# Swap, rope and split of dilated queries and keys by projection halves, with swap transfers issued by two engines

## The chip, the cores and the metric

One core of one Trainium2 chip runs the whole program. The metric is the device time of one execution, in microseconds. TensorE multiplies matrices into PSUM, VectorE and ScalarE work on rows of up to 128 partitions, GpSimd does the same more slowly, and SyncE does nothing here but issue transfers (ScalarE may issue them too).

## The reference, cut to what matters

Two layers run one after the other on 1024 tokens of width 1024. The second one has, beside a latent attention, a dilated one with 24 heads in three groups of 8. The change is in how its queries and keys are prepared:

```python
DIL_CONFIGS = ((128, 1), (512, 4), (2048, 16))      # window, dilation of group g

def rope(t, positions):
    ...
    t1, t2 = t[..., : dim // 2], t[..., dim // 2:]
    rot = jnp.concatenate([-t2, t1], axis=-1)
    return t * cos + rot * sin

def dilated_mixture(q, k, v, positions):
    q = rope(q.reshape(B, S, DIL_HEADS, DIL_HEAD_DIM), positions)
    k = rope(k.reshape(B, S, DIL_HEADS, DIL_HEAD_DIM), positions)
    ...
    for g, (window, dilation) in enumerate(DIL_CONFIGS):
        o, lse = dilated_group(q[:, :, sl], k[:, :, sl], v[:, :, sl], dilation, window // (2 * dilation))
    ...
    alpha = jax.nn.softmax(jnp.stack(lses, axis=0), axis=0)
    out = jnp.sum(alpha[..., None] * outs, axis=0)
```

Group g sees the tokens sorted by their remainder modulo the dilation (1, 4, 16), each remainder a band of its own. The head width is 64.

## The kernel before

All products are in float32 precision, made of three products of float32r parts: an operand is split into a high part (`hi`, a cast by ScalarE) and the rest (`lo`, a subtraction by VectorE, `sub_lo` in line 119). A projection of 128 channels by 512 tokens is 24 matmuls (lines 360 to 362), which need no other engine while they run.

The dilated stage is twelve units, g outermost: units 0 to 3 are g = 0, 4 to 7 are g = 1, 8 to 11 are g = 2. A unit is two heads, 128 channels on the partitions. Its three items in the stream of projections are key, query and value, each in two halves of 512 tokens. `q_evac` and `k_evac` take such a half out of PSUM; `ordered` copies it on ScalarE into the tile `rt` (128 x 1024), with the tokens sorted by remainder for g > 0 (half 0 and half 1 then interleave in blocks of 512 / dilation columns). After the second half, `roped` runs on the whole tile: four transfers copy `rt` with its 32-partition blocks exchanged in pairs into `rsw`, and VectorE computes rt * cos + rsw * sin in three steps. `split2` then casts and subtracts for each of the two heads (64 partitions each), into `qs` or `ksd`; for the keys two more transfers copy `ksd` onto the other 64 partitions. After this the scores of the unit (lines 1179, 1180) may run.

What sets the order: TensorE's instructions are put in order by a planner in the kernel (class `Flow`). It has lanes for scores (`score_lane`), transposes (`turn_lane`), values (`value_lane`) and the stream of projections, and each step of a lane waits for planned times: a lane is taken up when its events have come by the planner's own costs. `F.chain(("v", 1.3), ...)` adds a VectorE step of 1.3 us to the plan, and returns its end, which becomes `kev.t` or `qev.t`, the events that the scores of the unit wait for. Transfers cost SWAP = 4.5 us from the copy on, whichever engine issues them. The other engines' instructions are put in order by the framework's scheduler. The tiles `rt` and `rsw` come from a pool of six (`C`, with the planner's ring `R.C`), `qs` and `ksd` from pools of three.

All transfers signal their end on eight semaphores that go round (DMAHW0 to DMAHW7): one that is to use a semaphore first waits, on the engine that issues it, until the one before on that semaphore has landed.

Of the kernel before, what the change touches and what calls it, by code (L numbers as in the profile page):

```python
# [8 lines left out]
F32R = mybir.dt.float32r  # L9
# [5 lines left out]
S = 1024  # L15
# [52 lines left out]
def hybrid_kernel(  # L68
# [46 lines left out]
    def C(name="c", dt=F32):  # L115
        return cp.tile([128, 1024], dt, tag="c", name=name)
# [1049 lines left out]
    class Unit:  # L1166


        def __init__(self, j, g):
            self.j, self.g = j, g  # L1170
            self.kev, self.qev, self.vev = Ev(), Ev(), Ev()
            self.heads = [self.head(i) for i in range(2)]

# [33 lines left out]

        def roped(self, box, ps, half):

            if not half:  # L1210
                if self.j == 0 and not hasattr(self, "ks"):
                    tabs[0] = tables(self.g)
                box += [C("rt"), R.C.take()]
            t = box[0]
            e = self.ordered(t, ps, half)
            if half:
                cosT, sinT = tabs[0]
                sw, slot = C("rsw"), R.C.take()
                for b in range(4):
                    nc.sync.dma_start(sw[32 * b:32 * b + 32], t[32 * (b ^ 1):32 * (b ^ 1) + 32])  # L1220
                nc.vector.tensor_tensor(out=sw, in0=sw, in1=sinT, op=ALU.mult)  # L1221
                nc.vector.tensor_tensor(out=t, in0=t, in1=cosT, op=ALU.mult)
                nc.vector.tensor_tensor(out=t, in0=t, in1=sw, op=ALU.add)
                slot.t = F.chain(("v", 1.3), ("v", 1.3), ("v", 1.3), at=e + SWAP)
                box.append(slot.t)
            return e

        def split2(self, dst, t, at):

            for i in range(2):  # L1230
                r = slice(64 * i, 64 * i + 64)
                hi, lo = dst(i)
                nc.scalar.copy(hi, t[r])
                sub_lo(nc.vector, lo, t[r], hi)
            return F.chain(("a", 1.1), ("v", 1.3), ("v", 1.3), at=at)

        def q_evac(self):
            box = []

            def f(half):  # L1240
                def g(ps):
                    e = self.roped(box, ps, half)
                    if half:
                        self.qs = [dq.tile([128, S], F32R, tag="qs", name="qs") for i in range(2)]
                        self.qev.t = self.split2(lambda i: (self.qs[i][64 * i:64 * i + 64], self.qs[i][64 - 64 * i:128 - 64 * i]), box[0], box[2])
                        box[1].t = self.qev.t
                    return e
                return g
            return f

        def k_evac(self):
            box = []

            def f(half):
                def g(ps):
                    e = self.roped(box, ps, half)
                    if half:
                        self.ks = [dq.tile([128, 2, S], F32R, tag="ks", name="ksd") for i in range(2)]
                        t = self.split2(lambda i: [self.ks[i][64 * i:64 * i + 64, n] for n in range(2)], box[0], box[2])
                        for i in range(2):  # L1260
                            nc.sync.dma_start(self.ks[i][64 - 64 * i:128 - 64 * i].bitcast(F32), self.ks[i][64 * i:64 * i + 64].bitcast(F32))
                        box[1].t = t
                        self.kev.t = t + 4.0
                    return e
                return g
            return f
# [619 lines left out]
```

## Time and profile before

| | us |
|---|---|
| median of 3 runs | 1724.4 |
| lowest, highest of them | 1714.8, 1727.25 |
| the profiled execution, its own time | 1715.64 |
| its span in the trace | 1713.8 |
| TensorE busy | 1643.7 |
| VectorE, ScalarE busy | 980.1, 769.3 |

The profile is of one execution, and what lies between its span and its time is 1.8 us. A TensorE that is busy is not one at its peak; where it is idle, the profile names the engine and the line that ended the wait last. The dilated stage lies between about 417 and 1016 us.

### The profile page before, as it was taken

What the parts mean: (1) busy time and instruction counts of PE and PEld (TensorE: products, weight loads), DVE (VectorE), ACT (ScalarE), POOL (GpSimd) and SP (SyncE); (2) the same over time, 40 slices, a digit from 0 to 9 for tenths busy, and PEclk for the clock granted to TensorE, in tenths of its full rate; (3) what the DMA queues carried; (4) which work ended last, traced back from release to release, by engine and by line L of the source; (5) the groups of instructions that cost most, each with busy time, mean ns of one, the idle gap of its engine ahead of it and who ended that gap; (6) DMA issues with size and microseconds to landing.
All of it is one profiled execution on the core that took longest, in us unless ns stands there. A gap on an engine that the chain in (4) does not pass through costs nothing.

```text
span 1713.8 us, 22215 instructions
## 1 busy us (share of the span) xinstructions
PE 1643.7 (96%) x7988; PEld 1354.5 (79%) x7988; DVE 980.1 (57%) x1875; ACT 769.3 (45%) x1611; POOL 235.9 (14%) x224
## 2 busy tenths in 40 slices
PE   6999998999999899999999989999999999999998
PEld 6888876788788788888888777888777777777886
DVE  6487694553565656666555563374556566435433
ACT  5365524332455546555454542214566555632121
POOL 2000020000000010000000444451112122012200
PEclk8999999999999999999999999999999999999999
DMA  6211224534433343444334668455314132378542
GB/s 190 56 50 39 69 87 131 173 111 135 98 94 87 84 111 85 99 96 120 94 91 111 165 172 225 91 163 156 101 46 114 51 105 70 96 258 268 173 136 76
DMA packets 216090, 200.52 MB, mean 117 GB/s; under 512 B 49779, under 2 KB 180211, under 8 KB 214444
## 3 DMA queue, kind: packets, MB, share of 16 engines
q1 hardware_dynamic: 212844, 188.55, 40.0%
q10 hardware_dynamic: 3136, 10.55, 1.9%
q8 instruction: 63, 1.03, 0.3%
q14 instruction: 47, 0.39, 0.1%
HBM read 124.70 MB, written 48.07 MB: 101 GB/s over the span
## 4 chain that ended last, share of the span: by engine, by line
PE 70%; DMA 10%; DVE 6%; SPq 4%; ACT 4%; issue 3%; POOL 2%; DVEq 0%; POOLq 0%; ACTq 0%
PE pp L360 12%; PE pp L361 12%; PE pp L362 12%; PE y L361 3%; PE y L362 3%; PE y L360 3%; PE pso L493 3%; DMA rsw<-rt 3%; PE pst L463 2%; SPq L1220 2%; PE pso L1698 2%; PE pss L1655 2%; PE pso L1684 2%; PE pss L1657 2%; PE pss L1656 2%
## 5 line engine op out<-in xcount | busy, mean ns | idle before, releaser
L360 PE MATMUL pp<-Hh,whi 128*128 128x512 f32 x1248 | 503.7, 404 | 10.2 <-DVE pg L594 4.5
L361 PE MATMUL pp<-Hl,whi 128*128 128x512 f32 x1248 | 491.1, 394 | 0.0
L362 PE MATMUL pp<-Hh,wlo 128*128 128x512 f32 x1248 | 490.7, 393 | 0.0
L360 PEld LDWEIGHTS pp<-Hh,whi 128*128 128x128 f32 x1248 | 237.6, 190 | 56.7 <-DVE pg L594 5.5
L362 PEld LDWEIGHTS pp<-Hh,wlo 128*128 128x128 f32 x1248 | 236.5, 190 | 52.1
L361 PEld LDWEIGHTS pp<-Hl,whi 128*128 128x128 f32 x1248 | 237.4, 190 | 41.9
L119 DVE TENSOR_TENSOR wlo<-wraw,whi 128x1024 fp32r<-128x1024 f32 (+1 forms) x108 | 131.3, 1215 | 100.6 <-ACT whi L127 95.4
L127 ACT CAST whi<-wraw 128x1024 fp32r<-128x1024 f32 (+1 forms) x108 | 109.1, 1010 | 174.4 <-PE pp L361 77.3
L443 ACT ACTIVATE P<-P,nm 128x256 f32<-128x256 f32 (+2 forms) x256 | 118.6, 466 | 58.9 <-DVE nm L438 58.5
L119 DVE TENSOR_TENSOR pl<-pss,E 128x512 fp32r<-128x512 f32 x128 | 86.3, 688 | 91.5 <-ACT E L1663 91.0
L1662 ACT ACTIVATE pss<-pss 128x512 f32<-128x512 f32 x128 | 74.1, 582 | 111.4 <-PE pss L1657 102.2
L1599 DVE TENSOR_REDUCE mx<-pst 128x1 f32<-128x512 f32 x128 | 82.7, 684 | 32.0 <-PE pst L1597 31.5
L119 DVE TENSOR_TENSOR pl<-pst,ph 128x512 fp32r<-128x512 f32 (+2 forms) x120 | 75.2, 638 | 33.1 <-ACT ph L469 32.5
L432 DVE CUSTOM_DVE_ANT_0 P<-pss,cc 128x256 f32<-128x256 f32 (+2 forms) x192 | 63.0, 369 | 44.3 <-PE pss L1180 44.2
L469 ACT CAST ph<-pst 128x512 fp32r<-128x512 f32 (+2 forms) x120 | 63.8, 550 | 32.9 <-PE pst L463 31.9
L1663 ACT CAST E<-pss 128x512 fp32r<-128x512 f32 x128 | 72.8, 586 | 1.9
L493 PE MATMUL pso<-pl,v 128*128 128x256 f32 (+1 forms) x280 | 71.0, 284 | 2.3 <-DVE pl L119 2.3
L1221 DVE TENSOR_TENSOR rsw<-rsw,tab 128x1024 f32<-128x1024 f32 x24 | 29.4, 1224 | 73.1 <-DMA rsw<-rt 73.1
L493 PE MATMUL pso<-ph,v 128*128 128x256 f32 (+1 forms) x280 | 71.0, 283 | 0.2 <-ACT ph L469 0.2
L463 PE MATMUL pst<-idt,P 128*128 128x128 f32 x440 | 67.4, 274 | 2.6 <-ACT P L443 2.3
L502 ACT COPY ot<-pso 64x512 f32<-64x512 f32 x64 | 37.4, 584 | 70.2 <-PE pso L493 69.5
L1179 PE MATMUL pss<-ksd,qs 128*128 128x256 f32 (+2 forms) x192 | 50.0, 287 | 15.2 <-DVE qs L119 15.2
(262 smaller groups left out, 2999.1 us busy)
## 6 DMA issues: line engine op xcount, KB each, us to landing
wraw<-in_w_in_dram SPq DMA_DIRECT2D x78, 512.0 KB
rsw<-rt SPq DMA_DIRECT2D x96, 128.0 KB
ksd<-ksd SPq DMA_DIRECT2D x24, 512.0 KB
wraw<-in_w_out_dram SPq DMA_DIRECT2D x16, 512.0 KB
g_d<-g ACTq DMA_DIRECT2D x16, 512.0 KB
og_d<-ot SPq DMA_DIRECT2D x48, 128.0 KB
ol<-og_d SPq DMA_DIRECT2D x24, 256.0 KB
ol<-b_d SPq DMA_DIRECT2D x48, 128.0 KB
```

Of the source, the lines that this page charges most:

```text
L119: eng.tensor_tensor(out=lo, in0=src, in1=hi.bitcast(F32), op=ALU.subtract)
L127: nc.scalar.copy(wh, raw)
L360: nc.tensor.matmul(ps, lh, rh, start=(i == 0), stop=False)
L361: nc.tensor.matmul(ps, lh, rl, start=False, stop=False)
L362: nc.tensor.matmul(ps, ll, rh, start=False, stop=(i == n - 1))
L443: nc.scalar.activation(out=a, in_=a, func=AF.Exp, bias=nm[:, i:i + 1], scale=hd.scale, accum_out=hd.den[:, i:i + 1])
L463: nc.tensor.transpose(ps[:, w:w + 128], hd.P[i // 4][:, i % 4, p0:p0 + 128], ident)
L469: nc.scalar.copy(ph[:, :w], ps[:, :w])
L493: nc.tensor.matmul(o[b][:, q0:q0 + 128 * w], hd.v(c), part[:, cols + 128 * x:cols + 128 * (x + w)], start=b not in opened, stop=(part is p ...
L1599: nc.vector.tensor_reduce(out=mx[:, n, i:i + 1], in_=ps, axis=mybir.AxisListType.X, op=ALU.max)
L1662: nc.scalar.activation(out=ps, in_=ps, func=AF.Exp, scale=MSC)
L1663: nc.scalar.copy(ph, ps)
```

## The change

For g = 0 and g = 1 (`by_half`), everything that `roped` and `split2` do is done for each half as soon as that half has been copied: transfers of 32 x 512 in place of 32 x 1024, VectorE's and ScalarE's steps on 512 columns (`places` picks the half's columns; for g = 1 these are four blocks of 128). `rsw`, `qs` and `ksd` are taken at the first half. The planner's costs of the steps become 0.7 in place of 1.1 and 1.3. For g = 2 the whole tile is handled as before. For all three groups the four transfers of a swap are issued by SyncE and ScalarE by turns. The copies of `ksd` onto the other partitions stay as they were, after the second half.

```diff
--- before.py
+++ after.py
@@ -1167,7 +1167,7 @@
 
 
         def __init__(self, j, g):
-            self.j, self.g = j, g
+            self.j, self.g, self.by_half = j, g, g < 2
             self.kev, self.qev, self.vev = Ev(), Ev(), Ev()
             self.heads = [self.head(i) for i in range(2)]
 
@@ -1207,32 +1207,47 @@
 
         def roped(self, box, ps, half):
 
+
             if not half:
                 if self.j == 0 and not hasattr(self, "ks"):
                     tabs[0] = tables(self.g)
                 box += [C("rt"), R.C.take()]
             t = box[0]
             e = self.ordered(t, ps, half)
-            if half:
+            if self.by_half and not half or half and not self.by_half:
+                box += [C("rsw"), R.C.take()]
+            if half or self.by_half:
+                sw, v = box[2], self.places(half)
+                for b in range(4):
+                    (nc.sync, nc.scalar)[b % 2].dma_start(v(sw[32 * b:32 * b + 32]), v(t[32 * (b ^ 1):32 * (b ^ 1) + 32]))
                 cosT, sinT = tabs[0]
-                sw, slot = C("rsw"), R.C.take()
-                for b in range(4):
-                    nc.sync.dma_start(sw[32 * b:32 * b + 32], t[32 * (b ^ 1):32 * (b ^ 1) + 32])
-                nc.vector.tensor_tensor(out=sw, in0=sw, in1=sinT, op=ALU.mult)
-                nc.vector.tensor_tensor(out=t, in0=t, in1=cosT, op=ALU.mult)
-                nc.vector.tensor_tensor(out=t, in0=t, in1=sw, op=ALU.add)
-                slot.t = F.chain(("v", 1.3), ("v", 1.3), ("v", 1.3), at=e + SWAP)
-                box.append(slot.t)
+                nc.vector.tensor_tensor(out=v(sw), in0=v(sw), in1=v(sinT), op=ALU.mult)
+                nc.vector.tensor_tensor(out=v(t), in0=v(t), in1=v(cosT), op=ALU.mult)
+                nc.vector.tensor_tensor(out=v(t), in0=v(t), in1=v(sw), op=ALU.add)
+                us = 0.7 if self.by_half else 1.3
+                at = F.chain(("v", us), ("v", us), ("v", us), at=e + SWAP)
+                if half:
+                    box[3].t = at
+                box.append(at)
             return e
 
-        def split2(self, dst, t, at):
-
+        def places(self, half):
+
+            if not self.by_half:
+                return lambda ap: ap
+            m = 512 // RES[self.g]
+            return lambda ap: grouped(ap, self.g)[:, :, m * half:m * half + m] if self.g else ap[:, tokens(half)]
+
+        def split2(self, dst, t, at, half):
+
+            v = self.places(half)
             for i in range(2):
                 r = slice(64 * i, 64 * i + 64)
                 hi, lo = dst(i)
-                nc.scalar.copy(hi, t[r])
-                sub_lo(nc.vector, lo, t[r], hi)
-            return F.chain(("a", 1.1), ("v", 1.3), ("v", 1.3), at=at)
+                nc.scalar.copy(v(hi), v(t[r]))
+                sub_lo(nc.vector, v(lo), v(t[r]), v(hi))
+            us = 0.7 if self.by_half else 1.3
+            return F.chain(("a", us), ("v", us), ("v", us), at=at)
 
         def q_evac(self):
             box = []
@@ -1240,10 +1255,12 @@
             def f(half):
                 def g(ps):
                     e = self.roped(box, ps, half)
+                    if half == (not self.by_half):
+                        self.qs = [dq.tile([128, S], F32R, tag="qs", name="qs") for i in range(2)]
+                    if half or self.by_half:
+                        t = self.split2(lambda i: (self.qs[i][64 * i:64 * i + 64], self.qs[i][64 - 64 * i:128 - 64 * i]), box[0], box[-1], half)
                     if half:
-                        self.qs = [dq.tile([128, S], F32R, tag="qs", name="qs") for i in range(2)]
-                        self.qev.t = self.split2(lambda i: (self.qs[i][64 * i:64 * i + 64], self.qs[i][64 - 64 * i:128 - 64 * i]), box[0], box[2])
-                        box[1].t = self.qev.t
+                        self.qev.t = box[1].t = t
                     return e
                 return g
             return f
@@ -1254,9 +1271,11 @@
             def f(half):
                 def g(ps):
                     e = self.roped(box, ps, half)
+                    if half == (not self.by_half):
+                        self.ks = [dq.tile([128, 2, S], F32R, tag="ks", name="ksd") for i in range(2)]
+                    if half or self.by_half:
+                        t = self.split2(lambda i: [self.ks[i][64 * i:64 * i + 64, n] for n in range(2)], box[0], box[-1], half)
                     if half:
-                        self.ks = [dq.tile([128, 2, S], F32R, tag="ks", name="ksd") for i in range(2)]
-                        t = self.split2(lambda i: [self.ks[i][64 * i:64 * i + 64, n] for n in range(2)], box[0], box[2])
                         for i in range(2):
                             nc.sync.dma_start(self.ks[i][64 - 64 * i:128 - 64 * i].bitcast(F32), self.ks[i][64 * i:64 * i + 64].bitcast(F32))
                         box[1].t = t
```

In the order of TensorE, the first place that moves is unit 0: what stands ahead of its first scores (`pss<-ksd,qs`), the end of a projection of the next unit and the transposes of values (`pst<-idt,vt`).

```order
-L360 MATMUL pp<-Hh,whi 128x512
-L361 MATMUL pp<-Hl,whi 128x512
-L362 MATMUL pp<-Hh,wlo 128x512
-L518 MATMUL pst<-idt,vt 128x128 x8
 L1179 MATMUL pss<-ksd,qs 128x192
 L1180 MATMUL pss<-ksd,qs 128x192
```

Four more groups of three matmuls ahead of the rows shown go the same way: the scores move up past 15 matmuls of a projection and the 8 transposes, which now come later. In unit 3, 36 wide matmuls (384 or 512 columns) and 22 narrower ones stand between the query's second half and the first scores before, and 21 and 23 now.

On ScalarE, the second half of unit 3's queries: from the copy out of PSUM (`rt<-pp`) to the casts of the split (`qs<-rt`), with the high parts of P (`ph`), an output (`ot`) and the values' copy (`vt`) between. Before:

```order
L1205 COPY rt<-pp 128x512
L502 COPY ot<-pso 64x512
L469 CAST ph<-pst 128x512 x3
L1280 COPY vt<-pp 128x512
L1233 CAST qs<-rt 64x1024 x2
L502 COPY ot<-pso 64x512
L469 CAST ph<-pst 128x128
```

and now:

```order
L1205 COPY rt<-pp 128x512
L469 CAST ph<-pst 128x512
L1222 DMA rsw<-rt 32x512 x2
L469 CAST ph<-pst 128x512
L502 COPY ot<-pso 64x512
L469 CAST ph<-pst 128x128
L1299 COPY vt<-pp 128x512
L469 CAST ph<-pst 128x384
L1247 CAST qs<-rt 64x512 x2
```

Two transfers come in behind the copy, and the casts are of the second half alone (those of the first half stand ahead of this piece).

On SyncE, the key tile of unit 11 (g = 2): `st_d` and `cx` are the store and the twelve reads of the statistics of unit 10's heads, `d_d` the store of a merged output, which waits for GpSimd. Before, with the semaphores that a row waits for:

```order
L1320 DMA st_d<-sT 96x128 [waits DMAHW2_49,Activation_49]
L1384 DMA d_d<-acc 128x1024 [waits DMAHW3_49,Pool_49]
L1220 DMA rsw<-rt 32x1024 [waits DMAHW4_49,Activation_49]
L1220 DMA rsw<-rt 32x1024 [waits DMAHW5_49]
L1220 DMA rsw<-rt 32x1024 [waits DMAHW6_49]
L1220 DMA rsw<-rt 32x1024 [waits DMAHW7_49]
L1334 DMA cx<-st_d 16x64 [waits DMAHW2_49,DMAHW0_49]
L1337 DMA cx<-st_d 16x4x16 [waits DMAHW1_49]
```

and now:

```order
L1356 DMA cx<-st_d 16x16x4 [waits DMAHW0_49]
L1353 DMA cx<-st_d 16x64 [waits DMAHW1_49]
L1356 DMA cx<-st_d 16x4x16
L1403 DMA d_d<-acc 128x1024 [waits DMAHW3_49,Pool_49]
L1356 DMA cx<-st_d 16x16x4 [waits DMAHW4_49]
L1353 DMA cx<-st_d 16x64 [waits DMAHW5_49]
L1356 DMA cx<-st_d 16x4x16 [waits DMAHW6_49]
L1356 DMA cx<-st_d 16x16x4 [waits DMAHW7_49]
L1222 DMA rsw<-rt 32x1024 [waits DMAHW1_49,Activation_49]
L1222 DMA rsw<-rt 32x1024 [waits DMAHW3_49]
```

Ahead of the second piece stand the store of the statistics and five more reads. The swap has gone behind all twelve reads and the store of the output, and is two transfers. ScalarE's order at the same place, now:

```order
L1203 COPY rt<-pp 128x16x32 [waits PE_49]
L469 CAST ph<-pst 128x512 [waits PE_49]
L1222 DMA rsw<-rt 32x1024 [waits DMAHW2_49,DMAHW3_49,DMAHW1_49,DMAHW4_49,DMAHW0_49,DMAHW7_49,Activation_49,Pool_49]
L1222 DMA rsw<-rt 32x1024 [waits DMAHW2_49]
L443 ACTIVATE P,st<-P,nm 128x128 [waits DVE_49]
```

The other two transfers of the swap stand here, and wait for DMAHW0 and DMAHW2, the semaphores of the sixth and the eighth read.

## Rows read from the trace of the kernel before

**Rows 1.** The page, part 1: busy us, share of the span, instructions

```profile
PE 1643.7 (96%) x7988; PEld 1354.5 (79%) x7988; DVE 980.1 (57%) x1875; ACT 769.3 (45%) x1611; POOL 235.9 (14%) x224
```

**Rows 2.** Waits of TensorE, 410 to 815 us: us, times, longest us

```profile
PE pss L1179 <- DVE qs L119: 8.0, 4, 3.9
PE pst L518 <- ACT vt L1283: 2.3, 1, 2.3
```

**Rows 3.** The same, 815 to 1020 us

```profile
PE pss L1179 <- DVE qs L119: 7.3, 3, 3.8
...
PE pso L493 <- DVE pl L119: 1.1, 1, 1.1
```

**Rows 4.** Windows of 25 us: busy us (instructions) by engine, PEclk, DMA, GB/s

```profile
400.00:425.00 25.00, 25.00 (x115) 20.53 (x115) 7.74 (x10) 6.60 (x11) 0.71 (x2) 1.00 0.38 110
575.00:600.00 25.00, 20.74 (x102) 17.85 (x103) 13.57 (x31) 10.72 (x28) 0.15 (x1) 0.86 0.27 64
...
975.00:1000.00 25.00, 21.08 (x102) 17.42 (x102) 18.53 (x32) 11.64 (x22) 5.06 (x7) 0.93 0.79 188
```

**Rows 5.** Chain of waits, 573 to 590 us: start us, us, what

```profile
573.10 0.58 ACT rt L1205
...
574.30 1.51 SPq L1220
...
576.49 4.34 DMA rsw<-rt
...
580.95 1.22 DVE rsw L1221
...
583.91 1.14 DVE rt L1223
...
585.13 1.05 ACT qs L1233
...
586.20 1.23 DVE qs L119
...
587.48 0.53 PE pss L1179
```

**Rows 6.** Chain of waits, 410 to 1020 us

```profile
431.14 2.32 DMA rsw<-rt
...
485.98 1.16 PE pso L493 x10
...
971.77 1.81 DMA cx<-st_d
```

**Rows 7.** Tile rt: SyncE's swap transfers, duration ns min/median/max

```profile
L1220 SPq DMA_DIRECT2D rsw<-rt x96: 512/588/2192, 429.2 to 984.6; - x96
```

**Rows 8.** Tile g: transfers issued by ScalarE, duration ns min/median/max

```profile
L1048 ACTq DMA_DIRECT2D g_d<-g x16: 321/326/348, 1115.2 to 1525.9; - x16
```

**Rows 9.** VectorE by line and shape, 420 to 1016 us: count, busy, mean ns, idle before

```profile
L119 DVE TENSOR_TENSOR pl<-pst,ph 128x512 fp32r<-128x512 f32 x70 | 47.2, 683 | 27.6 <-ACT ph L469 27.5
...
L119 DVE TENSOR_TENSOR qs<-rt,qs 64x1024 fp32r<-64x1024 f32 x24 | 30.3, 1261 | 12.6 <-ACT qs L1233 12.2
...
L1221 DVE TENSOR_TENSOR rsw<-rsw,tab 128x1024 f32<-128x1024 f32 x24 | 29.4, 1224 | 73.1 <-DMA rsw<-rt 73.1
```

**Rows 10.** ScalarE by line and shape, 420 to 1016 us

```profile
L502 ACT COPY ot<-pso 64x512 f32<-64x512 f32 x45 | 26.3, 584 | 48.9 <-PE pso L493 48.4
...
L1233 ACT CAST qs<-rt 64x1024 fp32r<-64x1024 f32 x24 | 25.1, 1045 | 66.3 <-DVE rt L1223 66.0
```

**Rows 11.** Timeline of SyncE's transfers, 905 to 970 us

```profile
912.13 0.34 SPq L1334 DMA_DIRECT2D cx<-st_d  x1
...
916.34 0.89 SPq L1337 DMA_DIRECT2D cx<-st_d  x2
...
957.42 0.38 SPq L1320 DMA_DIRECT2D st_d<-sT  x1
```

## The prediction

> **What bounds the kernel now.** The page's first part comes first: TensorE is busy for 1643.7 of 1713.8 us [rows 1], so all that any change of order can win is the 70.1 us in which it stands, and what its clock loses. The change touches only the dilated stage, from about 417 us (first projection of its keys) to 1016 us. So I read TensorE's own waits there, apart for the two first groups of the units (g = 0 and 1, units 0 to 7, to 815 us) and the last one (g = 2, units 8 to 11). In both one wait leads: the first scores of a unit wait for VectorE's last step on the queries, 8.0 us in four waits and 7.3 us in three [rows 2, 3]. The rest of each list is short (2.3 us for the values, 1.1 us for a low part). The third view is the clock: of its two levels, 2.4 and 1.2 GHz, the lower was granted for part of the stretches around the longest of these waits (mean 0.86 in 575 to 600 us, 0.93 in 975 to 1000 and likewise in 850 to 875) [rows 4]. 25 us times the missing shares is 3.5 + 1.75 + 1.75 = 7.0 us at most. So what is to be won is 15.3 + 7.0 = 22.3 us, 1.3% of the time.
>
> Then the chain of such a wait, in unit 3 [rows 5]: ScalarE ends the copy of the second half at 573.68; SyncE issues four swap transfers until 576.49 (one took 1.51 us); they are there for VectorE 4.34 us later; three VectorE steps on 1024 columns end at 585.05; ScalarE's cast 1.05, VectorE's subtraction 1.23; the scores start at 587.48, 13.8 us after the copy. TensorE's cover for these 13.8 us is the work that stands between the projection and the scores. In the order before that is 36 matmuls of 384 to 512 columns and 22 narrower ones in unit 3. At 25.00 us for 115 wide ones [rows 4] and 1.16 us for ten narrow ones [rows 6] it is 36 x 0.22 + 22 x 0.116 = 10.5 us. The lack of 3.3 us beside the 3.9 us wait [rows 2] says that this reckoning holds. Counted in the same way, the cover of the 12 units before is 16.1, 16.8, 11.8, 10.5, 15.5, 15.3, 16.4, 15.1 and, for g = 2, 15.1, 14.2, 18.0, 16.2 us.
>
> **The change, part by part.**
>
> *The chain in halves (units 0 to 7).* For a half, the transfers on each queue are two: 2 x 0.59 = 1.2 us of issue by the median of the swap's own transfers [rows 7]. Landing: between 2.32 and 4.34 us after the last issue [rows 6, 5]. VectorE on 512 columns: no row shows it with both operands in SBUF; the same operation with one operand in PSUM takes 683 ns at 512, against 1224 and 1261 ns at 1024 [rows 9]; bounds 0.61 (half of 1224) and 0.68, and I take 0.68, a row of the operation itself. Three of them 2.05, up to 0.6 of other work between (the three of unit 3 took 4.1 us for 3.6 of work [rows 5]). Cast 0.58 [rows 10], subtraction 0.68, hops 0.3. Sum: 1.2 + 2.3 + 2.05 + 0.58 + 0.68 + 0.3 = 7.1 us to 1.2 + 4.3 + 2.65 + 1.56 = 9.7 us, in place of 13.8.
>
> *The order of TensorE* moves with it, since the planner reckons with the shorter steps: it puts scores earlier, and so takes away cover. The count in the new order gives 11.9, 13.7, 12.1, 7.3, 11.8, 13.7, 14.3, 14.3 us for units 0 to 7. Against 7.1 to 9.7 only unit 3 can still wait, 0 to 2.4 us; I take 1.0. Of the 8.0 us 7.0 go.
>
> *Two queues for all units.* For g = 2 halves are not used, so here only the issue changes: 1.2 us instead of four transfers, of which one in a query tile is held to about 2.2 us (maximum 2.192 [rows 7]). The cover becomes 15.3, 15.7, 15.7, 15.7, while issue falls by 1.2 to 3.5 us. Of the 7.3 us I take 6.0 as gone; the 3.8 us one had a cover that my reckoning calls nearly enough already, and may have another reason.
>
> The Trainium skill speaks against this part: "DMA: Bandwidth & Descriptors", section "Issuing engines are not separate DMA queues", says that a second issuing engine saves only the sequencer's own time, which is usually small beside the transfer. Here the traced issue is not small (1.51 us for one of four transfers beside 4.34 us of landing [rows 5]); by the rule the landing stays, as in my sum; what it would do to the held transfers is a rival below.
>
> *Clock.* If these waits go, so do most of the low stretches: 5.0 of 7.0 us, as unit 3's may stay in part. Gain so far: 7.0 + 6.0 + 5.0 = 18 us.
>
> *What ScalarE pays.* 80 transfers are now issued by ScalarE (64 for units 0 to 7, 16 for g = 2). Its own issue takes 0.326 us, SyncE's of the same swap 0.588 [rows 8, 7]: 26 to 47 us more in some 600, on an engine that is busy for 45% of the span [rows 1]. The halved casts are 32 more instructions, 16 x 2 x (2 x 0.584 - 1.05) = 4 us [rows 10, 5]. What hides this: ScalarE already stands 66.3 us in front of the query casts, waiting for VectorE [rows 10], with everything behind it, and the longest that TensorE waits for ScalarE is 2.3 us [rows 2]. Queued behind a transfer are the copies out of PSUM, the exponentials and the high parts of P. The bounds are 0 and 26 us (every one of 80 issues, 0.326 each, straight into TensorE). The nearest rows are the small waits that stand there today, so I take 4.
>
> *Transfers that ScalarE must wait for.* All transfers share eight completion semaphores (DMAHW0 to 7) in turn, and a transfer waits until the last one on its semaphore has landed. Until now that wait was SyncE's; now half of it stands in ScalarE's order. In most places the earlier transfer is over 5 us back. The exception is the key tile of units 10 and 11, where the twelve small statistics reads (cx) are issued just ahead: ScalarE waits for the sixth and eighth of them. In unit 10 the first read went out at 912.13 and the eighth by 916.8 [rows 11]; one lands 1.81 us after its issue [rows 6]. So ScalarE can be held there for 918.6 - 912.1 = 6.5 us if its copy is done when the reads start, and for nothing if it comes late; unit 11, whose statistics left at 957.42 [rows 11], has the same steps. Of this TensorE hides at least the 24 matmuls (5.3 us) that fill its other projection bank. Bounds 0 and 2 x 6.5 = 13; I take 3, what is left when the half of it is hidden and the copy comes midway.
>
> *VectorE* gets 5 x 16 = 80 more instructions, 16 x 5 x (2 x 0.683 - 1.22) = 12 us more work in 600, beside 73.1 us in which it stands today for swap transfers [rows 9]. It will stand for them 40 times instead of 24. Bounds 0 and 5 us of TensorE; 1 taken, since its waits for VectorE's other results are short today (1.1 us) [rows 3]. SyncE loses 16 transfers: nothing.
>
> **The sum.** 18 - 4 - 3 - 1 = 10 us gained. The profiled execution took 1715.6 us (span 1713.8), so 1705.6 for one like it; it lies near the lower end of the three runs shown, whose median is 1724.4. Against the median: 1724.4 - 10 = 1714 us. A measurement of this kernel tells about 1% (17 us) from no change.
>
> **Rivals.**
> *1. ScalarE becomes the late engine (slower).* Its order is fixed; a swap transfer stands in it that waits for its copy, for the tile's last readers and for a semaphore that another transfer, still stuck in SyncE's queue, has to free. There are 40 pairs. If each costs TensorE 0.7 us (the issue of both, 2 x 0.326), that is 26 us, with two more low-clock stretches of 3.5 us it is 33, against a gain of 15: 1724.4 + 18 = 1742; range 1728 to 1755. For it: the copies out of PSUM are ScalarE's, and the planner counts no time for the transfers. Against it: the 66.3 us that ScalarE stands today [rows 10] with almost no harm. It decides from 18 us of new TensorE waits on.
> *2. The cover shrinks as fast as the chain (no change).* If the chain is nearer 11 to 13 us (the landing of smaller transfers not shorter, VectorE's steps held by other work), units 0, 2, 3 and 4 wait again, since their cover is 7.3 to 12.1: 1724, range 1719 to 1730. For it: in unit 3 cover goes from 10.5 to 7.3.
> *3. The queue change gives only issue time.* Held transfers (2.192 us) stay held, since all run on the same engines; g = 2 keeps about 4 of its 7.3 us and 3.5 us of clock: 1714 + 5 = 1719. This is what the skill's rule would make of it; no row can show it before.
> *4. All of it, and ScalarE pays nothing:* 1724.4 - 22 = 1702.
>
> **How the numbers follow.** Forecast (1707 to 1722) 0.45; rival 3, beside it, 0.13; rival 2 0.12; rival 1 0.18; rival 4 0.12. Slower by over 1% (above 1741) is over half of rival 1: 0.10; faster by over 1% (under 1707) is rival 4 and a tail of the forecast: 0.20; the rest 0.70. The range runs from 1697 (rival 4, with a run as low as those of before go) to 1738 (the middle of rival 1).
>
> **What would show it.** Right: TensorE's waits of scores on the queries fall from 15.3 us to under 4; copy to first score in unit 3 under 11 us; no low clock near that place; transfers on ScalarE of 0.3 to 0.6 us; TensorE's busy time unchanged. Wrong: new waits of TensorE on ScalarE's copies, exponentials or high parts over 10 us in sum, or ScalarE idle in front of swap transfers by more than 20 us; scores that still wait on queries in units 0, 2 or 4; swap transfers on SyncE still held to 2 us.

## The result, and the profile after

The changed kernel takes 1698.6 us (median) beside 1721.2 us for the kernel before on the same chip: a ratio of 0.9878, 95% interval 0.9846 to 0.9909. One of its four executions took 2021 us at a mean granted clock of 0.75 and is left out of the ratio, which here and below is the one on record and can lie 0.0015 off the quotient of two medians. A second series of five runs gave 1697.4 beside 1718.3, ratio 0.9873 (0.9853 to 0.9894). The profiled execution took 1699.4 us, its span 1697.4: 16.4 us less than the span of before, 1713.8.

The page's first part, in the order of [rows 1] (busy us, share of the span, instructions):

```profile
PE 1638.9 (97%) x7988; PEld 1351.9 (80%) x7988; DVE 991.5 (58%) x1955; ACT 776.5 (46%) x1643; POOL 235.6 (14%) x224
```

TensorE is busy for 4.8 us less than before, and stands for 58.5 us (1697.4 - 1638.9) instead of 70.1: 11.6 us less. Together that is the whole gain of 16.4. VectorE has the 80 instructions more that were forecast and 11.4 us more (12 were forecast), ScalarE 32 casts and 7 us more.

TensorE's waits in the dilated stage come next. From 410 to 815 us, where [rows 2] stand for before, the view has no row at all, so TensorE waits there neither for queries nor for a result of ScalarE. From 815 to 1020 us it has one, and that one is longer than its fellow in [rows 3]:

```profile
PE pss L1179 <- DVE qs L119: 10.6, 2, 6.3
```

The clock by windows of 25 us of the changed kernel (columns as in [rows 4]). It is at its upper level where unit 3 had cost it before, and at its lower one for part of the time after the two waits that are left, those of units 10 and 11:

```profile
575.00:600.00 25.00, 25.00 (x151) 21.96 (x150) 16.04 (x54) 16.80 (x49) 0.63 (x4) 1.00 0.38 96
...
925.00:950.00 25.00, 20.94 (x110) 18.41 (x111) 15.88 (x45) 13.07 (x36) 18.97 (x11) 0.86 0.70 172
...
975.00:1000.00 25.00, 18.73 (x98) 16.28 (x98) 17.59 (x44) 12.97 (x36) 16.26 (x11) 0.86 0.79 196
```

In windows of 100 us between 400 and 1100 the mean granted clock was 1.00, 0.97, 1.00, 1.00, 0.98, 0.97 and 0.95 before and is 1.00 five times, 0.93 and 0.97 now. The missing shares add up to 13 us before and 10 us after: 3 us given back.

The tile rt shows the new steps (duration ns min/median/max): the swaps on both queues, and the operations on 512 columns.

```profile
L1222 SPq DMA_DIRECT2D rsw<-rt x80: 507/592/2177, 424.4 to 971.4; - x80
L1222 ACTq DMA_DIRECT2D rsw<-rt x80: 514/602/2086, 424.4 to 965.6; - x80
```

ScalarE's issue of a swap takes as long as SyncE's (602 beside 592 ns), not the 326 ns of its other transfers [rows 8], and held ones of 2.1 us are now found on both queues. There are fewer of them: 6 of 160 issues took over 1.5 us, where 10 of 96 did before. On VectorE, by line and shape (count, busy us, mean ns, idle before), the 512-column steps cost what [rows 9] gave for them:

```profile
L119 DVE TENSOR_TENSOR qs<-rt,qs 64x512 fp32r<-64x512 f32 x32 | 22.0, 686 | 6.1 <-ACT qs L1247 5.3
L1226 DVE TENSOR_TENSOR rt<-rt,rsw 128x512 f32<-128x512 f32 x32 | 21.9, 684 | 0.3
```

Unit 3, whose chain stands in [rows 5], shows what the halves do. Its last copy (ScalarE, 571.59 us for 0.58) ends at 572.17. TensorE's score products on its timeline (start us, us, what):

```profile
577.08 0.25 PE L1179 MATMUL pss<-ksd,qs 128*128 128x192 f32 x1
...
577.91 0.28 PE L1180 MATMUL pss<-ksd,qs 128*128 128x256 f32 x1
581.64 0.39 PE L1179 MATMUL pss<-ksd,qs 128*128 128x256 f32 x1
```

and VectorE's last step on the same queries, of the first half and of the second:

```profile
570.23 1.41 DVE L119 TENSOR_TENSOR qs<-rt,qs 64x512 fp32r<-64x512 f32 x2
...
580.90 1.41 DVE L119 TENSOR_TENSOR qs<-rt,qs 64x512 fp32r<-64x512 f32 x2
```

The first eight score products start 4.9 us after the copy, 3.8 us before the subtractions of the second half have so much as begun. They read only the first half, whose subtractions had ended at 571.64 (570.23 + 1.41), before the second half was even copied. So the chain from the last copy to the last step, 10.1 us here (15.0 before), isn't what the first scores wait for in this unit.

Last, ScalarE. In the kernel before it stood in front of a query cast, with the next copy of values behind it (its timeline, unit 0; in brackets the idle time and what ended it):

```profile
452.81 2.11 ACT L1233 CAST qs<-rt 64x1024 fp32r<-64x1024 f32 x2 [8.04 <-DVE rt L1223]
...
456.32 0.22 ACT L1283 COPY vt<-pp 128x64 f32<-128x64 f32 x1
```

That copy is the one that TensorE waited 2.3 us for [rows 2]. In the changed kernel:

```profile
447.58 1.26 ACT L1247 CAST qs<-rt 64x512 fp32r<-64x512 f32 x2 [1.47 <-DVE rt L1226]
...
452.12 0.22 ACT L1302 COPY vt<-pp 128x64 f32<-128x64 f32 x1
```

The wait of 8.04 us is 1.47, and the one of TensorE is gone. The new order also has these transposes of values later, at 455.83 us, but that alone would not have been enough, since before the copy ended only at 456.54. In all, ScalarE stands 35.2 us in front of query casts instead of 66.3 [rows 10]. All of that comes from units 0 to 7 (39.2 to 7.8 us). In units 8 to 11, whose casts are not halved, it stands 27.4 us where it stood 27.1.

### The profile page after: what moved, and what is told of

The parts are those of the page before. It is cut to its first block, busy times and chain, and to the rows that moved or that the text cites. A ratio compares the mean times of both kernels' runs of the same rounds, so it can differ in the third digit from the quotient of the medians.

```text
span 1697.4 us, 22364 instructions
## 1 busy us (share of the span) xinstructions
PE 1638.9 (97%) x7988; PEld 1351.9 (80%) x7988; DVE 991.5 (58%) x1955; ACT 776.5 (46%) x1643; POOL 235.6 (14%) x224
## 4 chain that ended last, share of the span: by engine, by line
PE 79%; DMA 9%; DVE 4%; SPq 3%; issue 2%; POOL 2%; ACT 2%; POOLq 0%; DVEq 0%; ACTq 0%
PE pp L360 15%; PE pp L361 14%; PE pp L362 14%; PE pso L493 3%; PE y L361 3%; PE y L362 3%; PE y L360 3%; PE pst L463 3%; PE pso L1717 2%; PE pss L1674 2%; PE pso L1703 2%; PE pss L1676 2%; PE pss L1675 2%; PE pst L1616 2%; PE pso L1704 2%
## 5 line engine op out<-in xcount | busy, mean ns | idle before, releaser
L1224 DVE TENSOR_TENSOR rsw<-rsw,tab 128x512 f32<-128x512 f32 (+1 forms) x40 | 31.9, 797 | 58.2 <-DMA rsw<-rt 58.1
L167 POOL TENSOR_TENSOR rs<-ms,mhalf 128x1 f32<-128x1 f32 (+1 forms) x40 | 25.0, 625 | 265.6 <-DVE ms L165 265.4
```

## The experiments

The theory (H): the halves shorten the chain, the first scores need only one half, and the second queue adds little. Its rivals: the second queue does it (Q), or ScalarE's issuing costs something that hides part of the gain (R). The first four kernels were run beside 17 runs of the kernel before on one chip (median 1717.9), the next four and the last four on another, each time beside 11 (1718.1 and 1718.3). Each edit is against the changed kernel. TensorE's instructions stand in the changed kernel's order in all kernels that keep halves in just eight units (runs 1, 3, 4, 5, 10 and 11).

**1. Halves, all swaps on SyncE**

```
-  (nc.sync, nc.scalar)[b % 2].dma_start(v(sw[...]), v(t[...]))
+  nc.sync.dma_start(v(sw[...]), v(t[...]))
```

> The halves of the change are kept, and all four swap transfers of a half are issued by SyncE again. Theory H (the halves shorten the chain from the projection to the scores, the second queue adds little): TensorE's waits between 410 and 815 us stay under 2 us against 8.0 before, the waits of units 8 to 11 stay at 7 to 10 us, ratio to before 0.988 to 0.994. Theory Q (it is the second queue that takes the transfers out of SyncE's line): the swaps held for 2.1 us on SyncE come back, the waits of units 0 to 7 too (5 us or more), ratio 0.996 to 1.002. Theory R (ScalarE's issuing costs something in the changed kernel): with it gone the time is below the changed kernel's, ratio 0.985 or less.

Measured: 1699.7 us, ratio 0.9879 (0.9843 to 0.9915). Most of the gain is there without the second queue: by the ratios nearly all, by the medians 18 us of 21 (run 9). TensorE's waits, 410 to 1020 us:

```profile
PE pss L1179 <- DVE qs L119: 6.4, 2, 3.5
PE pso L493 <- DVE pl L119: 4.7, 3, 2.1
PE pp L360 <- DVE g L594: 1.1, 1, 1.1
```

No unit from 0 to 7 waits for its queries, as H has it. But 4.7 us of waits for low parts (pl) have come, which the changed kernel doesn't have (H had named no such wait). The reason is one engine further on. VectorE stands in front of its first rotation step until the swap lands, with whatever is behind it. At 767.43 us of this run that was 2.37 us, and three instructions behind stood a pl, for which TensorE waited 1.6 us at about 770 us:

```profile
767.43 0.69 DVE L1224 TENSOR_TENSOR rsw<-rsw,tab 128x512 f32<-128x512 f32 x1 [2.37 <-DMA rsw<-rt]
...
769.24 0.67 DVE L119 TENSOR_TENSOR pl<-pst,ph 128x512 fp32r<-128x512 f32 x1
```

VectorE's waits of this kind come to 72.6 us with one queue and 58.1 with two. Against these 4.7 us stand query waits in units 10 and 11 that are 4.2 us shorter (6.4 beside 10.6), so that the second queue's small effect here is the balance of two. R falls: with ScalarE's issuing gone the time is not lower, and in the changed kernel TensorE waits for no result of ScalarE between 410 and 1020 us.

**2. The two queues alone**

```
-  self.j, self.g, self.by_half = j, g, g < 2
+  self.j, self.g, self.by_half = j, g, False
```

with the planner's costs of before, so that TensorE's order is that of before.

> The second queue alone: swap transfers issued by SyncE and ScalarE by turns, rope and split of all units over the whole tile of 1024 tokens as before. Theory H: the chain loses only issue time and part of the held transfers (13.8 us from the last copy to the first score in unit 3 becomes 11 to 13), so that 2 to 5 of the 8.0 us of waits between 410 and 815 us stay; ratio 0.994 to 1.000. Theory Q: the waits of units 0 to 7 go, ratio 0.985 to 0.991. Theory R: ScalarE's issuing shows without the gain of the halves, ratio over 1.000.

Measured: 1714.4 us, ratio 0.9979 (0.9961 to 0.9997): 3.5 us, as H has it, not Q. The chain in unit 3 went from 13.8 to 13.5 us (H had 11 to 13), and TensorE still waits for queries in 410 to 815 us, a little over H's 2 to 5 us:

```profile
PE pss L1179 <- DVE qs L119: 5.3, 3, 3.6
PE pso L493 <- DVE pl L119: 4.0, 2, 3.7
```

**3. Halves, all swaps on ScalarE**

```
-  (nc.sync, nc.scalar)[b % 2].dma_start(v(sw[...]), v(t[...]))
+  nc.scalar.dma_start(v(sw[...]), v(t[...]))
```

> The halves of the change are kept, and all four swap transfers are issued by ScalarE: twice the suspected cost, and no swap stands behind SyncE's other transfers any more. Theory H: ScalarE's issuing costs TensorE nothing and the waits of units 10 and 11 (10.6 us in the changed kernel, where the third swap stands behind the b_d stores on SyncE) fall under 5 us; ratio 0.980 to 0.988. Theory R: ScalarE, with some 96 more issues at 0.6 us, comes late with score sums or PSUM evictions: TensorE waits for it 5 us or more between 410 and 1020 us, ratio 0.990 to 1.005. Theory Q (two queues in parallel are what matters): the chain is as long as with SyncE alone, waits of 5 us or more in units 0 to 7, ratio 0.996 to 1.002.

Measured: 1729.3 us, ratio 1.0061 (1.0037 to 1.0085): all of the gain is lost and more. H was wrong. The time is a little above R's range (0.990 to 1.005), and R's reason doesn't hold either. TensorE's waits, 410 to 1020 us:

```profile
PE pss L1179 <- DVE qs L119: 21.5, 8, 6.3
PE pso L493 <- DVE pl L119: 3.5, 2, 3.0
PE pso L493 <- ACT ph L469: 1.5, 1, 1.5
PE pst L463 <- ACT P L443: 1.3, 1, 1.3
...
PE pst L518 <- ACT vt L1302: 0.6, 1, 0.6
```

It waits for ScalarE's own results for 3.4 us (1.5 + 1.3 + 0.6). The 21.5 us are queries again, 17.3 of them in units 8 to 11. They are late because the swaps land late: in unit 10 ScalarE issues the four from 941.88 on, 4.79 us long, and VectorE gets them at 952.97, 6.3 us after the last issue:

```profile
952.97 1.23 DVE L1224 TENSOR_TENSOR rsw<-rsw,tab 128x1024 f32<-128x1024 f32 x1 [4.22 <-DMA rsw<-rt]
```

With SyncE alone that lag was 4.0 us in the same unit (last issue ended 918.96, rotation at 922.92). Over the eight tiles of units 8 to 11 the median lag is 5.6 us against 3.0, and over the 32 halves 3.3 against 1.7 (VectorE had stood idle for the transfer at all eight tiles, and at 25 and 23 of the halves). VectorE stands 91.7 us for swaps, against 72.6. Why one queue serves the same transfers later than the other stays open.

**4. Rope by halves, split over the whole tile**

```
-  v = self.places(half)
-  for i in range(2):
+  v = lambda ap: ap
+  for i in range(2 if half else 0):
```

> As the changed kernel, rope by halves and two queues, but the split of the first eight units' queries and keys into two parts is made over the whole tile, behind the rope of the second half. It tells whether the first scores gain from starting on the first half alone. Theory H: in unit 3, where the changed kernel has its first scores 4.9 us behind the copy of the last half, they now wait for the whole split: 9 to 11 us, TensorE waits there 1.5 to 4 us and in units 0, 1, 2 under 2 each; ratio 0.988 to 0.993. The rival (it is the length of the chain to the end alone, the cover suffices anyway): no wait over 0.5 us in units 0 to 7 and the ratio of the changed kernel, 0.986 to 0.989.

Measured: 1702.6 us, ratio 0.9896 (0.9870 to 0.9923). In unit 3 the first scores now come 10.9 us after the copy instead of 4.9. Of TensorE's waits in 410 to 815 us the first:

```profile
PE pss L1179 <- DVE qs L119: 5.4, 2, 4.6
```

The 4.6 us wait is unit 3's, a little over H's bound of 4, and low clock is back there (0.97 in 550 to 600 us). The median lies 4 to 5 us above the changed kernel's 1697.4 to 1698.6. That is what the start on the first half alone gives, as H has it, but the two intervals overlap, so the amount is likely and not certain.

**5. The coefficient stores on ScalarE.** In the changed kernel SyncE has these transfers in unit 10, behind the copy that ends at 912.64 (timeline, start us, us, what):

```profile
912.66 0.54 SPq L1222 DMA_DIRECT2D rsw<-rt  x1
913.31 1.35 SPq L1280 DMA_DIRECT2D ksd<-ksd  x1
914.74 4.18 SPq L1374 DMA_DIRECT2D b_d<-cw  x3
918.97 1.30 SPq L1222 DMA_DIRECT2D rsw<-rt  x1
```

Its second swap waits behind three stores, so that the issue ends at 920.27, 7.6 us behind the copy. Unit 11 has the same picture.

```
-  nc.sync.dma_start(b_d[j, g]..., e[:, g])
+  nc.scalar.dma_start(b_d[j, g]..., e[:, g])
```

> The changed kernel, but the three stores b_d<-cw of each coefficient block are issued by ScalarE instead of SyncE. In the changed kernel they stood 4.18 us long in front of the third swap transfer of units 10 and 11, and TensorE waited 10.6 us for these two units' queries. Theory S (that place in SyncE's line is the cause): the swaps' issue ends under 4 us behind the copy instead of 7.6 and 6.9, the waits of units 10 and 11 fall from 10.6 to 3 to 6 us in all (to what they are with all swaps on SyncE, 6.4 us, or below), and the time falls by 3 to 8 us: ratio 0.983 to 0.987. Rival T (the stretch is full of transfers, the landing is late whoever stores): the waits stay over 8 us, ratio 0.986 to 0.990. Rival R (ScalarE held by the stores comes late itself): new waits for ScalarE, ratio 0.989 or more.

Measured: 1697.4 us, ratio 0.9876 (0.9835 to 0.9917), waits of units 10 and 11 13.0 us. This told nothing apart, since the stores only changed the queue that they block. ScalarE's timeline in unit 10:

```profile
912.00 0.52 ACTq L1222 DMA_DIRECT2D rsw<-rt  x1
912.98 4.37 ACTq L1374 DMA_DIRECT2D b_d<-cw  x3
917.39 0.87 ACTq L1222 DMA_DIRECT2D rsw<-rt  x1
```

**6. Halves in all twelve units, two queues**

```
-  self.j, self.g, self.by_half = j, g, g < 2
+  self.j, self.g, self.by_half = j, g, True
```

> Rope and split by halves for the last four units too (g = 2), two queues as in the changed kernel. A half of such a tile is made of pieces of 32 tokens, 128 bytes, so that the swaps move many small pieces. If what shortened units 0 to 7 works here (from the last copy to the last score operand 8 to 11 us instead of 14.5 to 17.6, cover 12.0 to 13.8 us): TensorE's waits between 815 and 1020 us fall from 10.6 us to under 3, time 5 to 12 us below the changed kernel's, ratio 0.981 to 0.985. If the small pieces make the transfers late (landing 3 us or more behind the last issue, where halves in the other units took 2.0): waits stay at 6 to 12 us, ratio 0.986 to 0.991.

Measured: 1701.1 us, ratio 0.9888 (0.9852 to 0.9924). The query waits are gone, as expected, and nothing is gained. TensorE's waits, 410 to 1020 us:

```profile
PE pst L518 <- ACT sT L1337: 3.9, 2, 2.2
PE pso L493 <- DVE pl L119: 2.3, 1, 2.3
PE pp L360 <- DVE g L594: 1.5, 1, 1.5
PE pss L1179 <- DVE qs L119: 0.8, 1, 0.8
PE pp L360 <- ACT rt L1203: 0.6, 1, 0.6
```

Together 9.1 us instead of 10.6. Behind the stage, from 1020 to 1130 us, the wait for g is 6.0 us instead of 2.9, and the mean clock 0.92 instead of 0.97, which is 5.5 us in 110. It looks as if units 10 and 11 had been waiting for queries in a stretch where other work is late anyway.

**7. Halves in all twelve units, SyncE alone** (edits 1 and 6 together)

> Halves in all twelve units, all swaps issued by SyncE. Beside the run with halves in all units and two queues it asks once more what the second queue gives. Theory H (nothing): ratio within 0.003 of that run's, waits between 410 and 815 us 1 to 4 us as with SyncE alone before. Theory Q (with 16 more transfers on SyncE's line it matters now): at least 5 us slower than that run, new waits of units 8 to 11 for the swaps.

Measured: 1708.1 us, ratio 0.9939 (0.9920 to 0.9957), 7.1 us above run 6 (the two intervals just touch). Here Q is right and H wrong: TensorE waits 9.8 us for queries, where run 6 has 0.8, and VectorE stands 77.4 us for swaps against 58.7.

**8. Halves in all units, stores on ScalarE** (edits 5 and 6)

> Both together: halves in all twelve units with two queues, and the stores b_d<-cw issued by ScalarE. If both causes of the waits of units 8 to 11 are the right ones, no TensorE wait over 1 us between 410 and 1020 us for queries: ratio 0.978 to 0.983, the fastest of these kernels. If one of them already takes the whole wait, the ratio of the better of the two alone.

Measured: 1701.6 us, ratio 0.9894 (0.9858 to 0.9929). Query waits of 5.6 us in two units and no gain over run 6: the stores on ScalarE help as little here.

**9. The changed kernel again**

> The changed kernel once more, as the measure for the three kernels beside it: ratio 0.985 to 0.991; TensorE waits of about 10 us for the queries of units 10 and 11.

Measured: 1697.4 us (1697.2 to 1699.6), ratio 0.9873 (0.9853 to 0.9894); query waits of units 10 and 11 11.1 us. It stands for comparison with the three that follow.

**10. The stores on GpSimd**

```
-  nc.sync.dma_start(b_d[j, g]..., e[:, g])
+  nc.gpsimd.dma_start(b_d[j, g]..., e[:, g])
```

> The changed kernel with the stores b_d<-cw issued by GpSimd, so that they stand ahead of a swap transfer on neither SyncE nor ScalarE (on ScalarE they took the same place, 4.37 us ahead of its second swap). Theory S (a place behind the stores is what delays the swaps of units 10 and 11): issue ends under 4 us behind the copy instead of 7.6 and 6.9, waits of the two units 2 to 6 us instead of 10.6, time 3 to 8 us below the changed kernel's beside it. Rival T (the stretch is full of transfers, landing is late in any case): issue ends early, but the rotation still starts 9 us or more behind the copy, waits 8 us or more, time within 3 us of the changed kernel's. A third way: the waits go, and the time doesn't, since another chain ends the stage.

Measured: 1692.2 us (1687.6 to 1698.1), ratio 0.9845 (0.9818 to 0.9872), the lowest of all. SyncE's timeline in unit 10 shows the line cleared, with the issue ended at 916.03 instead of 920.27:

```profile
912.68 0.54 SPq L1222 DMA_DIRECT2D rsw<-rt  x1
913.32 1.34 SPq L1280 DMA_DIRECT2D ksd<-ksd  x1
914.71 1.32 SPq L1222 DMA_DIRECT2D rsw<-rt  x1
```

But VectorE's rotation there starts at almost the same time as with the stores in the way, 921.69 beside 921.99 in the changed kernel:

```profile
921.69 1.22 DVE L1224 TENSOR_TENSOR rsw<-rsw,tab 128x1024 f32<-128x1024 f32 x1 [6.92 <-DMA rsw<-rt]
```

So in unit 10 the place behind the stores was not what made the swaps late: T is right there, S wrong. In unit 11 the rotation came 8.2 us after the copy instead of 10.3 (run 9), so S has a part. Query waits fell to 8.5 us, not to 2 to 6. The medians differ by 5.2 us, the two profiled spans by 4.5 (1695.8 and 1691.3). The waits of the stage fell by 2.2 (11.1 against 8.5 + 0.4) and the wait for g behind it by 3.0 (3.3 against 0.3); why g came earlier wasn't followed up. The two intervals overlap, so that the 5 us are likely rather than certain.

**11. The same, all swaps on SyncE** (edits 1 and 10)

> The same stores on GpSimd, and all swaps issued by SyncE, rope by halves in the first eight units. Theory H (the second queue adds nothing): within 3 us of the run with two queues and the stores on GpSimd. Theory Q (the second queue was hidden by the stores in its way and shows once they are gone): 4 us or more slower than that run, waits of units 8 to 11 over 6 us where that run has under 6.

Measured: 1699.0 us, ratio 0.9884 (0.9862 to 0.9906), 6.9 us above run 10 (the intervals overlap by 0.001). That is Q's time. Its waits of units 8 to 11 are 9.0 against 8.5 us, so Q's place for it is wrong; the difference in the waits is again 4.2 us for pl, of which run 10 has none, and VectorE stands 74.7 us for swaps instead of 56.3.

**12. Halves in all units, stores on GpSimd** (edits 6 and 10)

> Halves in all twelve units, two queues, the stores on GpSimd. Halves in all units with two queues had left 0.8 us of query waits and yet was no faster than the changed kernel, since waits of 7 us for sT, pl and g and low clock of 13.7 us behind the stage came in their place. If the stores on SyncE and ScalarE have part in that: 4 us or more below the changed kernel's time beside it, ratio 0.980 to 0.985. If the end of the stage is set by the coefficient blocks' own chain: ratio 0.986 to 0.991 as all the others, with waits of 5 us or more between 1000 and 1130 us.

Measured: 1699.8 us, ratio 0.9887 (0.9866 to 0.9908), as the second way had it: 4.6 us of waits for g behind the stage and 3.0 for sT, where the query waits are 1.8.

What the planner's new costs do by themselves, with the work left whole, was not tried.

## Why the prediction was right, and where it was off

The time came out inside the range and near its lower end, 15 us under the figure of 1714; the gain of 1.2% is just beyond the 1% at which the text draws the line to faster, to which it gave 0.20. Three things make up the 15 us. The base was the median of three runs, 1724.4; over the longer series it is 1718, so 6 us of it are the base. Another 6 are the sum: 16.3 us gained between the profiled executions instead of 10. The last 3 lie between the profiled executions and the medians, within the spread of the runs. Of the signs that the text named, copy to first score in unit 3 (4.9 us) and the clock there came true, but the waits for queries fell from 15.3 us to 10.6 and not to under 4. By its terms:

| term | forecast | measured in the profiles |
|---|---|---|
| query waits, units 0 to 7 | -7.0 | -8.0 (8.0 to 0) |
| query waits, units 8 to 11 | -6.0 | +3.3 (7.3 to 10.6) |
| clock | -5.0 | -3 |
| ScalarE's issues and holds | +4 and +3 | -4.3 (2.3 + 0.2 + 1.8 to 0) |
| VectorE | +1 | -1.5 (0.4 + 1.1 to 0) |
| sum | -10 | -13.5; the other 2.9 of the span lie outside this list |

The two largest misses are of opposite sign: what ScalarE pays came out 11.3 us better than forecast, the query waits of units 8 to 11 came out 9.3 us worse. That the sum is off by 3.5 us only is luck.

*The halves* did what the text said. The steps cost what it took for them (684 to 689 ns against 0.68 us; cast 619 against 584 ns, subtraction 686), and the chain to the last step shrank to 8.2 to 10.7 us in units 0 to 7. Run 1 shows that this alone brings a ratio of 0.9879. What it missed is that the first scores need only the first half, as unit 3 shows. So even this unit, with a cover of 7.3 us (4.9 of it behind the copy) against a chain of 10.1, doesn't wait; run 4 puts that at some 4 us.

*The step that was mis-sized most is what ScalarE pays*: +7 in the sum, -4.3 in the profile. The 66.3 us that it stood in front of query casts [rows 10] were taken as cover with almost no harm. In unit 0 they were the harm: the copy of values for which TensorE waited 2.3 us stood behind such casts, and went early when the casts did. The other 1.8 us, in unit 10, went in another way. There ScalarE stands longer in front of the casts than before (timelines of before and of the changed kernel, with the copies of values behind):

```profile
942.68 2.12 ACT L1233 CAST qs<-rt 64x1024 fp32r<-64x1024 f32 x2 [4.96 <-DVE rt L1223]
```

```profile
926.71 2.11 ACT L1247 CAST qs<-rt 64x1024 fp32r<-64x1024 f32 x2 [8.95 <-DVE rt L1226]
```

The copy behind them now ends at 930.51, and TensorE comes to its transposes only at 932.22, after 4.35 us of waiting for the queries: this wait has hidden the other. That the issue is 0.60 and not 0.33 us did not matter beside it. The expected hold behind the statistics reads in units 10 and 11 did not come: ScalarE's two swaps there took 1.16 us together in the key tile of unit 10 and 1.38 in that of unit 11. Rival 1 has its price seen in run 3, where ScalarE issues all swaps and the kernel is 0.6% slower than before, but by late landing more than by ScalarE's lateness (17.3 us of query waits in units 8 to 11 beside 3.4 us for ScalarE).

*The query waits of units 8 to 11* were to shrink by 6 us through the second queue. In units 8 and 9 they went (1.7 and 1.8 us to 0; the chain to the last step fell from 17.0 and 16.2 to 14.5 and 14.7 us), but so they did in run 1, without the second queue. In units 10 and 11 they grew from 0 and 3.8 to 4.35 and 6.3 us. The step that failed is the cover. The text counts it in TensorE's work from the end of the projection on (15.7 us, the 63 wide and 16 narrow matmuls that stand between it and the first scores) and sets it against a chain that begins with ScalarE's copy, and ScalarE's copy is late in these two units. In unit 10 the projection's last matmul ends at 908.58 us; the copy stands behind the key's casts, which wait for VectorE, and begins 3.5 us after it (TensorE's and ScalarE's timelines):

```profile
908.19 0.39 PE L362 MATMUL pp<-Hh,wlo 128*128 128x512 f32 x1
...
929.06 0.47 PE L1179 MATMUL pss<-ksd,qs 128*128 128x128 f32 x1 [4.35 <-DVE qs L119]
```

```profile
908.96 2.12 ACT L1247 CAST ksd<-rt 64x1024 fp32r<-64x1024 f32 x2 [3.19 <-DVE rt L1226]
...
912.06 0.58 ACT L1203 COPY rt<-pp 128x512 f32<-128x512 f32 x1
```

In unit 11 it is 5.5 us (projection to 959.00, copy from 964.46), in units 8 and 9 only 0.8. So TensorE has 12.1 and 10.1 us of work left behind the copy, where units 8 and 9 have 14.2 and 14.6, and the scores start 16.4 us behind it. The same was so before: in unit 11 the copy came 7.4 us after the projection and left 10.6 us of cover, not the 16.2 of the text, which explains the 3.8 us wait that it left with "another reason". Rival 3 was right that these waits stay, but not by its own reason: issues held over 1.5 us are found in the query tiles of units 8 and 9, and none in those of units 10 and 11.

*The second queue.* The Trainium skill's rule in "DMA: Bandwidth & Descriptors", section "Issuing engines are not separate DMA queues", says that a second issuing engine saves only the sequencer's time. For run 2 (3.5 us of 1718) and for run 1 beside the changed kernel (1 to 2 us, within the spread of the runs) the runs agree. In the two other pairs, runs 7 and 6 and runs 11 and 10, one queue costs 7 us more, with VectorE standing 18 us longer at its rotations and other results queued behind them. That the sequencer's time, small in itself, is paid there through VectorE fits the waits, but is argued: in run 1 VectorE stands 14.5 us longer as well, and the time hardly differs. Rival 4's time (1702) was nearest to the measured one, for partly other reasons than its own.

*What stays open*: why the swaps of units 10 and 11 land late. In the changed kernel VectorE's rotation starts 9.4 and 9.3 us after the copy there, in units 8 and 9 7.3 and 7.0. Run 10 excludes the stores as the cause in unit 10. In the changed kernel, in run 1 and in run 10 the rotation there starts 10.1 to 10.9 us after the first of two key copies of 512 KB went out on SyncE (911.59, 912.07 and 911.60 us; rotation at 921.99, 922.92 and 921.69). That fits landing behind these copies, but the record speaks against it as well: in units 8 and 9, which do not wait, the same distance is 9.6 and 10.4 us, in unit 10 of run 5 it is 12.7, and in unit 11 of run 3 the swaps went out ahead of the key copies (from 995.25, the copies from 998.09) and were taken up 10.9 us after ScalarE's copy all the same. It's not shown.

## What to carry to other kernels

Cutting a chain of small steps into halves pays twice where the consumer can start on the first half: look at which part the first consumer reads, beside the length of the chain. Count the cover from the instruction that starts the chain: where that copy itself stands in a queue behind another wait, part of the cover is gone before it begins. An engine that stands idle in front of a step isn't cover by that alone: look at what is queued behind the step, and whether TensorE waits for that. Before a transfer is moved to another queue, look at when it lands, and not only at when it is issued.

## What was not expected of the hardware

- A swap's issue took 0.60 us on ScalarE and 0.59 on SyncE, where ScalarE's transfers of 512 KB to DRAM took 0.33 [rows 8].
- With all four swaps on ScalarE's queue VectorE took them up later behind their last issue than with all on SyncE's: 5.6 against 3.0 us (medians over eight whole tiles, runs 3 and 1), 3.3 against 1.7 (over 32 halves).
- Held issues of 2.1 to 2.2 us are found on either queue (2.18 on SyncE, 2.09 on ScalarE in the changed kernel). GpSimd's issue of the three small stores in unit 10 took 1.74 us, where SyncE's took 4.18 and ScalarE's 4.37.
